# Hybrid attention layer on one core: the last query chunk's projection tiles move from the four-buffer PSUM pool "S" to the two-buffer pool "O"

## The chip, the core and the metric

The kernel runs on one core of a Trainium2 chip. The metric is the time of one execution on the device in microseconds (us). One profiled execution of the kernel before is read in detail; the rows below are from it.

## The reference, cut to what matters

One decoder layer on 512 tokens of width 1024. A normalised and modulated input `h` is projected by `w_in` into the operands of two attention groups of eight heads: NSA (query `q_n`; compressed, selected and windowed keys and values) and DSA (query `q_d`; one key and value head, and an index branch that picks 128 keys per query). Their outputs go through `w_out`, and a squared-ReLU MLP follows.

```python
h = rms_norm(x, g_pre_mix) * (1 + sc1) + sh1
proj = h @ w_in
q_n, kc, vc, ksl, vsl, kw, vw, gl, q_d, k_d, v_d, qi, ki, wi = split(proj)
k_cmp = gelu(blocks(rope(kc)) @ w1k) @ w2k          # and v_cmp from vc
o_nsa = g0 * attn(q_n, k_cmp, v_cmp) + g1 * attn_selected(q_n, ksl, vsl) + g2 * attn_window(q_n, kw, vw)
o_dsa = attn_on_topk(q_d, k_d, v_d, index(qi, ki, wi))
x = x + gt1 * rms_norm(concat(o_nsa, o_dsa) @ w_out)
x = x + gt2 * rms_norm(square(relu(h2 @ w_up)) @ w_down)
```

## The kernel before, in words

The 512 tokens are four tiles of 128 (index `t` or `j`). The columns of `w_in` are cut into chunks: A and B are projected first, together with the modulation vectors; then D, C (the NSA queries) and E (the DSA queries, "the last query chunk"). Each fp32 operand is split into a high and a low part, so a projection of one tile is 8 x 3 = 24 matmuls of 128x512 into one PSUM bank.

PSUM has eight banks, given out by `bank(tag, name)` (L112) from three pools: "S" has four buffers, "T" and "O" two each. A tile from a pool waits until the last reader of the tile that held the buffer is done. Pool "S" holds the projection tiles of D, C and E (`pj_D`, `pj_C`, `pj_E`), the index products (`ix`), the score tiles (`s_s`, `s_w`, `s_d`, and `sc` of the compressed branch), the sums `vs_g`, `gv_g`, and `cv_a`. Pool "T" holds the transposes (`skp_C`, `skp_E`, `tp_...`). Pool "O" holds, before the attention, the transposed compression inputs (`kcT`, `vcT`) and the hidden layer of the compression (`hid_k`, `hid_v`, L649), and in the attention the output accumulators `O0_j` and `O1_j` (L1124).

A tile of chunk C or E goes through four steps: `Q0` (the 24 matmuls; for E `Q0_steps`, four parts), `Q1` (ScalarE copies the bank to SBUF as `pjC` or `pjE`, L555; VectorE and GpSimd rotate one half each, L428 to L433, with the scratch `ra_C`), `Q2` (split into stacked high and low parts `sk_C`: a ScalarE cast, L437, and a GpSimd subtract, L438), `Q3` (eight transposes `skp_C` and two ScalarE copies to `qC`, L569).

The compression of the values: `kcp_v` (L643, VectorE) feeds 16 matmuls `hid_v` (L653), VectorE copies the bank out (`hx`, L660), a short chain on VectorE and ScalarE makes the GELU `hu` (L661 to L666), and `cout_v` (L674) follows. The same for the keys ends in `kcx` (L681 to L684), which `sc` (L961) reads.

The attention is a list of units (kind s, w or d; tile j). For each head a unit makes a score tile in "S" by two matmuls (L912, L913) which VectorE reads with the mask (L915, result `P_s` and the maxima `mx`), then ScalarE exponentiates (L916). Meanwhile VectorE runs the rounds of the top-k on `wk` (`MAX8` L594, `MATCH_REPLACE8` L597, 16 rounds for each of three tiles).

Where pieces of work lie in the program is set by the table `PLAN` (L41) through `place` and `slot`: chunk E at `E=(19, 2.5)` falls into the first three attention units (s of tile 0, w of tile 0, s of tile 1). The framework's scheduler then fixes the order of the instructions on each engine; each engine runs its own queue strictly in that order.

Of the kernel before, what the change touches and what calls it, by code (L numbers as in the profile page):

```python
# [69 lines left out]
def layer_kernel(  # L70
# [41 lines left out]
    def bank(tag, name, dt=F32):  # L112
        return psp.tile([P, 512], dt, tag=tag, name=name, bufs=4 if tag == "S" else 2)
# [180 lines left out]
    def mod_mm(k):  # L294
        ps, acc = macc[k]
        for v in range(2):
            mm = PE.matmul(ps[:, 256 + v:257 + v], acc[:, v, :], ones32, start=True, stop=True)
        return ps[:, 256:258], mm
# [28 lines left out]
    def proj_mm(ps, t, k, w, n):  # L327
        for i in range(3):
            proj_pass(ps, t, k, w, n, i)
# [27 lines left out]
    mp, _ = mod_mm(0)  # L357
# [105 lines left out]
    pjs, sks = {}, {}  # L463
# [81 lines left out]
    def Q0_steps(nm, t):  # L545
        def part(i):
            if i == 0:
                pjs[nm, t] = bank("S", f"pj_{nm}_{t}")
            for k in (2 * i, 2 * i + 1):
                proj_mm(pjs[nm, t], t, k, chunks[nm], 512)  # L550
        return [lambda i=i: part(i) for i in range(4)]
# [9 lines left out]
    def Q2(nm, t):  # L561
        rv = heads(pjs[nm, t], 8)
        sks[nm, t] = [stack(rv[:, g * 4:g * 4 + 4, :], 4, f"{nm}{t}{g}", G) for g in range(2)]

    def Q3(nm, t):
        q = b4(f"q{nm}_{t}", F32R).rearrange("p (h q) -> p h q", q=P)
        for g in range(2):
            ps = stack_T(sks[nm, t][g], 4, f"{nm}{t}{g}")
            A.copy(q[:, g * 4:g * 4 + 4, :], ps.rearrange("p (h q) -> p h q", q=P))  # L569
        (qn if nm == "C" else qd)[t] = q  # L570
# [224 lines left out]
    def w_in_chunk(c0, c1, nm, eng=V):  # L795
# [7 lines left out]
        def spl(i):  # L803
# [13 lines left out]
            lambda t, nm=nm: Q2(nm, t), lambda t, nm=nm: Q3(nm, t)), t) for t in range(NT) for nm in "C"]  # L817
# [53 lines left out]
    for n in range(len(tl) + 3):  # L871
# [5 lines left out]
        while mm_done < min(want, len(mm_seq)):  # L877
            f, t = tl[mm_seq[mm_done]]
# [230 lines left out]
    for n in range(16):  # L1109
# [7 lines left out]
        if prev is not None:  # L1117
            j, b = prev.j, int(prev.nm == "d")
            O = (On, Od)[b]
# [233 lines left out]
```

## Time and profile before

| quantity | value |
|---|---|
| median of 3 runs | 716.63 us (716.0 to 717.08) |
| profiled execution, its own time | 716.14 us |
| its span, first to last instruction | 714.4 us |
| outside the span | 1.7 us |
| TensorE (PE) busy / VectorE (DVE) / ScalarE (ACT) / GpSimd (POOL) | 93% / 73% / 52% / 27% of the span |
| mean granted TensorE clock | 0.977 |

PE is busy nearly all the time, but its busy time counts a matmul at half clock twice as long as one at full clock, and an idle stretch counts only where nothing runs. So the places to read are the idle stretches of PE and the stretches where the granted clock is 0.5.

### The profile page before, as it was taken

What the parts mean: (1) busy time and instruction counts of PE and PEld (TensorE: products, weight loads), DVE (VectorE), ACT (ScalarE), POOL (GpSimd) and SP (SyncE); (2) the same over time, 40 slices, a digit from 0 to 9 for tenths busy, and PEclk for the clock granted to TensorE, in tenths of its full rate; (3) what the DMA queues carried; (4) which work ended last, traced back from release to release, by engine and by line L of the source; (5) the groups of instructions that cost most, each with busy time, mean ns of one, the idle gap of its engine ahead of it and who ended that gap; (6) DMA issues with size and microseconds to landing.
All of it is one profiled execution on the core that took longest, in us unless ns stands there. A gap on an engine that the chain in (4) does not pass through costs nothing.

```text
span 714.4 us, 9896 instructions
## 1 busy us (share of the span) xinstructions
PE 662.9 (93%) x3465; PEld 519.1 (73%) x3465; DVE 522.6 (73%) x1027; ACT 371.7 (52%) x753; POOL 191.7 (27%) x228
## 2 busy tenths in 40 slices
PE   3899979989988999899978999999999999999994
PEld 2678968857665666455768878888888888888883
DVE  4557759997899999865686559657688559695535
ACT  4343784534697768644546454525545346444221
POOL 4000395624533226203010022202130022231023
PEclk9999989997999999999999999999999999999998
DMA  9998730521215421833496123361154212323103
GB/s 287 314 342 275 254 89 1 118 91 57 72 48 138 99 60 30 213 140 89 134 294 195 57 60 106 109 199 29 30 170 155 89 30 60 89 90 111 35 1 118
DMA packets 88539, 87.14 MB, mean 122 GB/s; under 512 B 3909, under 2 KB 67497, under 8 KB 88490
## 3 DMA queue, kind: packets, MB, share of 16 engines
q1 hardware_dynamic: 88098, 86.46, 40.3%
q8 instruction: 27, 0.44, 0.3%
q14 instruction: 22, 0.18, 0.1%
q10 hardware_dynamic: 392, 0.06, 0.0%
HBM read 84.40 MB, written 2.10 MB: 121 GB/s over the span
## 4 chain that ended last, share of the span: by engine, by line
PE 72%; DVE 16%; ACT 3%; DMA 3%; issue 2%; POOL 2%; DVEq 0%; POOLq 0%; ACTq 0%; SPq 0%
PE up L1154 23%; PE dn L1282 16%; PE dn L1215 5%; PE op L1045 4%; PE pA L324 3%; PE pj_E L324 3%; PE pB L324 2%; DVE wk L597 2%; PE O L944 2%; DVE m L594 2%; PE pj_D L324 1%; DMA wg_g<-in_w_ada_dram 1%; PE pj_C L324 1%; PE mp L286 1%; DVE uol_a L124 1%
## 5 line engine op out<-in xcount | busy, mean ns | idle before, releaser
L1154 PE MATMUL up<-hh,uh_U 128*128 128x512 f32 (+1 forms) x288 | 105.4, 367 | 3.2 <-ACT hh L123 2.7
L1154 PE MATMUL up<-hl,uh_U 128*128 128x512 f32 (+1 forms) x288 | 104.3, 366 | 1.5 <-DVE hl L124 1.5
L1154 PE MATMUL up<-hh,ul_U 128*128 128x512 f32 (+1 forms) x288 | 104.9, 366 | 0.0
L1244 POOL TENSOR_TENSOR r<-r,r 128x512 f32<-128x512 f32 x18 | 36.8, 2056 | 184.3 <-ACT r L1159 113.6
L123 ACT CAST th<-rd 128x1024 fp32r<-128x1024 f32 x42 | 44.2, 1053 | 75.1 <-PE dn L1282 40.7
L124 DVE TENSOR_TENSOR tl<-rd,th 128x1024 fp32r<-128x1024 f32 x42 | 54.0, 1291 | 37.8 <-ACT th L123 37.8
L124 DVE TENSOR_TENSOR ul_U<-rw_U,uh_U 128x1024 fp32r<-128x1024 f32 x32 | 43.1, 1348 | 31.2 <-ACT uh_U L123 31.1
L1154 PEld LDWEIGHTS up<-hh,uh_U 128*128 128x128 f32 x288 | 54.3, 188 | 12.7 <-ACT hh L123 3.2
L1154 PEld LDWEIGHTS up<-hl,uh_U 128*128 128x128 f32 x288 | 53.8, 189 | 10.6 <-DVE hl L124 1.7
L1154 PEld LDWEIGHTS up<-hh,ul_U 128*128 128x128 f32 x288 | 54.3, 188 | 8.7
L123 ACT CAST uh_U<-rw_U 128x1024 fp32r<-128x1024 f32 x32 | 33.6, 1049 | 49.3 <-PE up L1154 31.2
L1282 PE MATMUL dn<-th,sl 128*128 128x512 f32 x168 | 52.1, 391 | 0.3
L1282 PE MATMUL dn<-th,sh 128*128 128x512 f32 x168 | 51.9, 393 | 0.0
L1282 PE MATMUL dn<-tl,sh 128*128 128x512 f32 x168 | 51.8, 389 | 0.0
L1282 PEld LDWEIGHTS dn<-th,sh 128*128 128x128 f32 x168 | 31.5, 188 | 7.5 <-DVE usum L1269 0.6
L1282 PEld LDWEIGHTS dn<-th,sl 128*128 128x128 f32 x168 | 31.3, 188 | 7.6 <-DVE sl L124 1.2
L1282 PEld LDWEIGHTS dn<-tl,sh 128*128 128x128 f32 x168 | 31.5, 188 | 6.6
L1244 DVE TENSOR_TENSOR rd<-rd,rd 128x1024 f32<-128x1024 f32 x24 | 31.5, 1325 | 1.9 <-DMA rd<-in_w_down_dram 1.6
L123 ACT CAST sh<-r 128x512 fp32r<-128x512 f32 x42 | 25.2, 617 | 9.1 <-POOL r L1244 8.6
L124 DVE TENSOR_TENSOR sl<-r,sh 128x512 fp32r<-128x512 f32 x42 | 27.9, 713 | 0.0
L1269 DVE TENSOR_TENSOR y<-y,dn 128x512 f32<-128x512 f32 x40 | 25.5, 681 | 2.2 <-PE dn L1282 2.2
L594 DVE MAX8 m<-wk 128x8 f32<-128x256 f32 (+2 forms) x48 | 26.3, 553 | 0.8 <-POOL wk L589 0.4
(425 smaller groups left out, 1685.3 us busy)
## 6 DMA issues: line engine op xcount, KB each, us to landing
rw_U<-in_w_up_dram SPq DMA_DIRECT2D x32, 512.0 KB, 4.3
rd<-in_w_down_dram SPq DMA_DIRECT2D x24, 512.0 KB, 4.9
wm<-in_w_ada_dram SPq DMA_DIRECT2D x32, 256.0 KB, 6.1
x<-in_x_dram SPq DMA_DIRECT2D x8, 512.0 KB, 6.8
wa<-in_w_ada_dram SPq DMA_DIRECT2D x8, 512.0 KB, 7.9
wv_g<-in_w_ada_dram SPq DMA_DIRECT2D x8, 512.0 KB, 4.5
rwo_a<-in_w_out_dram SPq DMA_DIRECT2D x16, 256.0 KB, 4.3
wv_sh<-in_w_ada_dram SPq DMA_DIRECT2D x8, 512.0 KB, 3.8
```

Of the source, the lines that this page charges most:

```text
L123: A.copy(hi, src)
L124: eng.tensor_tensor(lo, src, hi.bitcast(F32), op=OP.subtract)
L324: return PE.matmul(ps[:, :n], l[:, t, k, :], r[:, k % 2, :n], start=(k == 0 and i == 0), stop=(k == KT - 1 and i == 2))
L594: mx = V.max(m8, work[t])
L597: V.match_replace(work[t], m8, work[t], MARK)
L944: mm = [PE.matmul(O[j][g * 64:(g + 1) * 64, :], vn[kb][:, self.vsl[g]:self.vsl[g] + 64], pts[kb, g][0], start=(first and kb == 0), stop=(l ...
L1045: PE.matmul(stt["ps"], l[:, kk, :], r[:, kk % 2, :], start=(kk == 0 and i == 0), stop=(kk == 7 and i == 2))
L1154: PE.matmul(pv[:, t0:t1, :], l[:, k, :], r[:, t0:t1, k, :], start=(n == 0), stop=(n == 23))
L1215: PE.matmul(ps, l[:, t * P:(t + 1) * P], r[:, f % 2, :], start=(n == 0), stop=(n == 11))
L1244: eng.tensor_tensor(dst, x, y, op=op)
L1269: V.tensor_tensor(ya, ya, ps, op=op)
L1282: PE.matmul(ps[t], l[:, f, t * P:(t + 1) * P], r[:, f, :], start=(n == 0), stop=(n == 11))
```

## The change

The bank of each `pj_E` tile is taken from pool "O" (two buffers) and no longer from pool "S" (four buffers). Nothing is computed otherwise.

```diff
     def Q0_steps(nm, t):
         def part(i):
             if i == 0:
-                pjs[nm, t] = bank("S", f"pj_{nm}_{t}")
+                pjs[nm, t] = bank("O", f"pj_{nm}_{t}")
             for k in (2 * i, 2 * i + 1):
                 proj_mm(pjs[nm, t], t, k, chunks[nm], 512)
```

The scheduler orders the instructions anew. The orders of all engines are as before up to the end of the `ix` products, and again from the second unit s of tile 0 on (apart from one or two neighbours that change places); between these PE, VectorE, ScalarE and GpSimd all run the same instructions in another order. By the waits in the built program, the first matmul of the first E tile waited before for an index bank (long free), and now waits for VectorE's copy L660 of `hid_v`, whose bank it takes; the first matmul of the second E tile waited before for a score bank, and now for the copy L660 of `hid_k`; the third takes the bank of the first, the fourth that of the second.

On PE, right after the last index products (`skp_kw_1491`), these rows stand new in front of the first E tile `pj_E_1688` (`skp_C_1534` and `skp_C_1540` are the transposes of the first C tile's halves, `s_s_0` to `s_s_3` the scores of the first four heads of the first attention unit).

```order
+L444 MATMUL skp_C_1534<-identr,sk_C_1418 128x128 x4
+L653 MATMUL hid_v<-kcp_v,w_v_905 128x62 x8
+L653 MATMUL hid_v<-kcp_v,w_v_907 128x62 x8
+L444 MATMUL skp_C_1540<-identr,sk_C_1421 128x128 x4
+L912 MATMUL s_s_0_1699<-k1s,qC_1533 128x128
+L913 MATMUL s_s_0_1699<-k2s,qC_1533 128x128
+L912 MATMUL s_s_1_1713<-k1s,qC_1533 128x128
+L913 MATMUL s_s_1_1713<-k2s,qC_1533 128x128
+L912 MATMUL s_s_2_1730<-k1s,qC_1533 128x128
+L913 MATMUL s_s_2_1730<-k2s,qC_1533 128x128
+L912 MATMUL s_s_3_1745<-k1s,qC_1533 128x128
+L913 MATMUL s_s_3_1745<-k2s,qC_1533 128x128
```

So the first E tile's 24 matmuls, which stood directly behind `skp_kw_1491` and surrounded `hid_v` and `skp_C`, now stand behind all of these.

On VectorE at the same time, right behind the rotation of the third C tile (L432 on `pjC_1473`), the copy of `hid_v` and the reads of the first scores move ahead (`wk_705` and `wk_704` are top-k work, `ra_C_1517` the rotation scratch of the fourth C tile).

```order
-L597 MATCH_REPLACE wk_705<-m_2_1672,wk_705 128x384
-L597 MATCH_REPLACE wk_704<-m_1_1675,wk_704 128x256
 L428 TENSOR_TENSOR ra_C_1517<-pjC_1515,rsin 128x4x32
 L430 TENSOR_TENSOR ra_C_1517<-pjC_1515,rsin 128x4x32
+L660 COPY hx<-hid_v 128x62
+L597 MATCH_REPLACE wk_705<-m_2_1672,wk_705 128x384
+L915 ISA P_s_1695,mx<-s_s_0_1699,mask 128x128
+L915 ISA mx 128x1
+L597 MATCH_REPLACE wk_704<-m_1_1675,wk_704 128x256
+L915 ISA P_s_1695,mx<-s_s_1_1713,mask 128x128
+L915 ISA mx 128x1
+L915 ISA P_s_1695,mx<-s_s_2_1730,mask 128x128
```

The copy of `hid_v` is now the third instruction from that point and was the eighth; the copy of `hid_k`, which the second E tile waits for, comes 25 instructions and accumulator reads behind that of `hid_v` (21 before).

On PE at the end of the third E tile (`pj_E_1814`), the sums `vs_g` close up and the two transposes of the first E tile (`skp_E_1942`, `skp_E_1948`) leave the place in front of `sc`; they come after the first two `s_w` scores now, behind `cv_a`.

```order
 L324 MATMUL pj_E_1814<-uh_E_1430,hl_173 128x512
-L749 MATMUL vs_g_1750<-wv_g_1903,c_sb 32x256
-L679 MATMUL cout_k_1626<-hu_1570,w2t_809 64x62
-L749 MATMUL vs_g_1750<-wv_g_1903,c_sb 32x256 x3
+L749 MATMUL vs_g_1750<-wv_g_1786,c_sb 32x256 x4
+L749 MATMUL vs_g_1750<-wv_g_1903,c_sb 32x256 x4
 L444 MATMUL skp_C_1654<-identr,sk_C_1582 128x128 x4
 L444 MATMUL skp_C_1660<-identr,sk_C_1585 128x128 x4
-L444 MATMUL skp_E_1942<-identr,sk_E_1808 128x128 x4
-L444 MATMUL skp_E_1948<-identr,sk_E_1811 128x128 x4
 L961 MATMUL sc_1833<-kcx,qC_1533 128x64 x8
 L827 MATMUL cv_a_1852<-ones,acc_a_187 128x1 x8
```

Between the last wide matmul of the third E tile and `cv_a` there is less narrow work than before; the fourth E tile still follows behind `cv_a`.

## Rows read from the trace of the kernel before

**Rows 1.** The page: the span, the busy time of each engine, and the shares of the chain of work that ended last.

```profile
span 714.4 us, 9896 instructions
...
PE 72%; DVE 16%; ACT 3%; DMA 3%; issue 2%; POOL 2%; DVEq 0%; POOLq 0%; ACTq 0%; SPq 0%
```

**Rows 2.** Busy time by stretch (start and end in us; length; busy us and count of PE, weight load, VectorE, ScalarE, GpSimd; granted clock; DMA share; GB/s).

```profile
150.00:160.00 10.00, 10.00 (x69) 6.60 (x68) 8.26 (x34) 3.56 (x12) 0.00 (x0) 1.00 0.43 144
160.00:170.00 10.00, 8.81 (x59) 6.65 (x57) 6.83 (x22) 4.17 (x10) 3.79 (x6) 0.98 0.38 120
170.00:180.00 10.00, 10.00 (x38) 9.09 (x39) 8.74 (x36) 3.68 (x15) 5.12 (x10) 0.51 0.00 0
180.00:190.00 10.00, 10.00 (x73) 7.64 (x75) 6.68 (x28) 5.33 (x16) 4.66 (x9) 1.00 0.01 2
```

**Rows 3.** The waits of PE over the whole span: who waited for whom, total us, times, longest us.

```profile
PE pj_E L324 <- DVE mx L915: 4.8, 1, 4.8
```

**Rows 4.** PE in order of time around the first and second E tiles (start us, us, engine, line, operation, names, shape, count, and the idle time before it with what ended it). The rows show each matmul's own time; matmuls overlap, so what one costs in a row of them is the distance from start to start.

```profile
130.41 0.28 PE L444 MATMUL skp_kw<-identr,sk_kw 128*128 128x128 f32 x2
...
133.12 1.99 PE L653 MATMUL hid_v<-kcp_v,w_v 128*128 128x62 f32 x16
134.86 0.90 PE L444 MATMUL skp_C<-identr,sk_C 128*128 128x128 f32 x8
135.59 2.05 PE L653 MATMUL hid_v<-kcp_v,w_v 128*128 128x62 f32 x16
...
139.75 0.22 PE L912 MATMUL s_s<-k1s,qC 128*128 128x128 f32 x1
...
140.14 0.45 PE L324 MATMUL pj_E<-uh_E,hh 128*128 128x512 f32 x1
...
146.00 0.80 PE L324 MATMUL pj_E<-uh_E,hh 128*128 128x512 f32 x1 [4.78 <-DVE mx L915]
146.60 0.63 PE L324 MATMUL pj_E<-ul_E,hh 128*128 128x512 f32 x1
...
148.30 0.63 PE L324 MATMUL pj_E<-uh_E,hl 128*128 128x512 f32 x1
...
149.11 0.39 PE L324 MATMUL pj_E<-ul_E,hh 128*128 128x512 f32 x1
...
151.64 0.39 PE L324 MATMUL pj_E<-uh_E,hh 128*128 128x512 f32 x1
```

**Rows 5.** VectorE in order of time, same stretch and columns.

```profile
131.79 0.68 DVE L643 TENSOR_TENSOR kcp_v<-kcp_v,peT 128x512 f32<-128x512 f32 x1
...
139.06 0.09 DVE L597 MATCH_VALUE_LOAD wk<-m,wk 128x8 f32 x1
...
139.99 0.60 DVE L428 TENSOR_TENSOR ra_C<-pjC,rsin 128x128 f32<-128x128 f32 x1
140.52 0.82 DVE L430 TENSOR_TENSOR ra_C<-pjC,rsin 128x128 f32<-128x128 f32 x1
...
142.85 0.21 DVE L660 COPY hx<-hid_v 128x62 f32<-128x62 f32 x1
...
150.06 0.21 DVE L660 COPY hx<-hid_k 128x62 f32<-128x62 f32 x1
```

**Rows 6.** ScalarE in order of time, same stretch and columns: the two halves of the first C tile, and the copy of the first E tile.

```profile
138.01 1.06 ACT L569 CAST qC<-skp_C 128x512 fp32r<-128x512 f32 x2
...
145.42 0.58 ACT L555 COPY pjE<-pj_E 128x512 f32<-128x512 f32 x1
```

**Rows 7.** The granted clock (third column from the right) in short stretches around its changes; columns as in rows 2.

```profile
146.00:149.00 3.00, 3.00 (x7) 2.43 (x8) 2.96 (x12) 1.86 (x8) 1.77 (x3) 0.50 0.00 0
164.50:169.50 5.00, 3.81 (x33) 2.60 (x32) 3.04 (x10) 2.20 (x6) 0.91 (x2) 1.00 0.32 105
169.50:179.50 10.00, 10.00 (x39) 9.16 (x39) 8.24 (x32) 4.18 (x16) 5.10 (x9) 0.50 0.00 0
179.50:180.00 0.50, 0.50 (x3) 0.43 (x2) 0.50 (x6) 0.00 (x0) 0.01 (x1) 0.74 0.00 0
```

**Rows 8.** PE in order of time at another start behind an idle stretch, in chunk C; columns as in rows 4.

```profile
103.17 0.80 PE L324 MATMUL pj_C<-uh_C,hh 128*128 128x512 f32 x1 [3.03 <-ACT rl L582]
...
107.60 0.61 PE L324 MATMUL pj_C<-ul_C,hh 128*128 128x512 f32 x1
```

**Rows 9.** PE in order of time from the last wide matmul of the third E tile to the fourth E tile; columns as in rows 4.

```profile
164.27 0.39 PE L324 MATMUL pj_E<-uh_E,hl 128*128 128x512 f32 x1
...
167.26 0.51 PE L444 MATMUL skp_C<-identr,sk_C 128*128 128x128 f32 x4 [0.77 <-ACT qC L569]
...
168.53 0.51 PE L444 MATMUL skp_E<-identr,sk_E 128*128 128x128 f32 x4 [0.42 <-ACT qC L569]
169.99 3.55 PE L827 MATMUL cv_a<-ones,acc_a 128*128 128x1 f32 x16
...
175.58 0.73 PE L324 MATMUL pj_E<-uh_E,hh 128*128 128x512 f32 x1
```

**Rows 10.** VectorE from 139 to 152 us, grouped by line and shape (count, busy us, mean ns of one, idle us before).

```profile
L597 DVE MATCH_REPLACE8 wk<-m,wk 128x384 f32<-128x384 f32 x6 | 3.3, 542 | 0.0
L594 DVE MAX8 m<-wk 128x8 f32<-128x384 f32 x5 | 2.7, 549 | 0.0
```

## The prediction

> **What bounds the kernel now.** I read the page first, for the chain that ended last: 72% of it is PE and 16% VectorE, so PE's idle and slow stretches are what can be won [rows 1]. Next the list of PE's waits: one wait of an E tile for VectorE's maxima, 4.8 us, stands in it [rows 3]. Then PE in order of time. The first E tile runs from behind `skp_kw` at 130.41 on, with `hid_v` and `skp_C` let in; its bank is read out late, because ScalarE's queue holds the copy until 145.42 [rows 4, 6]. The two scores after it sit unread in "S" while VectorE works through top-k rounds, and so the second E tile, next on PE, stands from 141.22 to 146.00 without a bank: 4.78 us [rows 4]. It then starts at half clock: steps of (148.30 - 146.60) / 4 = 0.43 us against (151.64 - 149.11) / 11 = 0.23 us, with the clock granted at 0.50 from 146 to 149 [rows 4, 7]. Last I read busy time by stretch, to see who follows: from 150 to 190 VectorE is idle for 1.74 + 3.17 + 1.26 + 3.32 = 9.5 us while PE is hardly ever idle [rows 2]. So over this region PE sets the pace, and what PE wins here VectorE can follow.
>
> **The change part by part.** No work is added or removed; the E tiles leave "S", and the scheduler reorders one region. I follow PE from the end of `skp_kw` (130.7) to where the order is as before, and count waits and half-clock time, since the work is the same.
>
> Removed: the wait of 4.78 us, and the slow start behind it. Seven matmuls at 0.43 instead of 0.23 cost 7 x 0.2 = 1.4 us [rows 4, 7]. Two small waits for ScalarE's evacuation of transposes, 0.77 and 0.42 us [rows 9], go too: `skp_C` now comes behind eight matmuls of `vs_g`, and `skp_E` behind `cv_a`. Together 7.4 us.
>
> Added, first wait: `skp_C` takes (135.59 - 134.86) / 2 = 0.37 us for four, and then `hid_v` needs `kcp_v`, which ends at 131.79 + 0.68 = 132.5 [rows 4, 5]. Before, eleven matmuls of the E tile filled this; now PE waits from 131.1 to 132.5: 1.4 us.
>
> Added, second wait: `hid_v` twice 1.74 us (134.86 - 133.12), `skp_C` 0.37 and four pairs of scores at (140.14 - 139.75) / 2 = 0.2 us each bring PE to 137.2 [rows 4]. The scores of the first four heads need only the first half of `qC`, whose copy now stands ahead of the casts on ScalarE; even at its old time, 138.01 plus half of 1.06 [rows 6], they would be done by 139.4. The first E tile then waits for the copy of `hid_v`. VectorE's queue is unchanged up to 139.06 [rows 5]; then come L428, L430 and the copy. Their old durations give 139.06 + 0.60 + 0.82 + 0.21 = 140.7; a later L428 and L430 in these rows' queue, without GpSimd on the same data, would be shorter, and at half of them the copy ends at 140.0. GpSimd does its own share of the third C tile earlier now, so I take 139.9: a wait of 2.7 us, between 2.2 and 3.5. Behind the waiting matmul on PE stand `vs_g`, the next scores and the second E tile; the top-k rounds cover VectorE meanwhile.
>
> Added, a slow start: PE has then seen 9 us of idling, transposes, 62-column and 128-column matmuls. Before, the clock fell during the 4.78 us of idling, and in another place in a stretch of narrow work that began behind the last wide matmul at 164.27 and stood at half from 169.5 [rows 7, 9]. I expect the first E tile to start at half clock. Seven slow matmuls are seen at 146.00, and eleven from 103.17 to 107.60 [rows 4, 8], so 1.4 to 2.2 us; I take nine, 1.8 us, since nothing favours either. The Trainium skill, "TensorE: Matmul & The Clock Gate", Part 1, says that the number of cold matmuls at a start varies with where in the chip's own rhythm the first one falls, and that one kernel showed 6, 11 or 14. The 7 and 11 here agree; 14 would be 2.8 us by that page, 1.0 us more than I take.
>
> The waits and slow starts so far: 1.4 + 2.7 + 1.8 - 7.4 = -1.5 us.
>
> The bank of the second E tile is freed by the copy of `hid_k`. Between the two copies stand 25 rows of VectorE's queue. Before, 21 rows took 150.06 - 142.85 = 7.2 us [rows 5]; with four more of 0.1 to 0.5 us this is 8 us, so 147.9. PE reaches that tile at 139.9 + 24 x 0.23 + 1.8 = 147.2 plus some 2.3 us of `vs_g`, three score pairs, `cout_v` and `skp_C`: 149.5. Cost nothing, with 1.6 us to spare.
>
> The second slow stretch: the clock was half from 169.5 to past 179.5, all of it with PE busy, which is half of 10.2 us, 5.1 us lost [rows 7]. It fell 5 us behind the last wide matmul (164.27 + 0.39), just as `cv_a` began, and rose some 4 us after the fourth E tile began at 175.58 [rows 9]. In the new order `skp_E` and two waits (0.73 + 0.77 + 0.42 = 1.9 us) leave the stretch between the third E tile and `cv_a`. If the clock falls as long after the last wide matmul as before, 1.9 us of the narrow work more runs at full clock and saves about half, 0.9 us; but `skp_E`, 0.73 us at full clock, moves into the slow part, while three score pairs move out behind wide matmuls. I take -0.9 us, between 0 (the clock falls that much earlier) and -1.7 (it also rises earlier, by a third of the 10.2 us).
>
> Sum: -1.5 - 0.9 = -2.4 us. From there on the order is as before, all engines have waited for PE in the region (9.5 us of slack on VectorE), and the transfers of `w_ada` and `w_out` are released by the same instructions, so the rest follows 2.4 us earlier. Against the profiled execution's own 716.14 us this is 713.7 us. That execution is 0.5 us below the median of the runs (716.63); I forecast 713.7 and leave the 0.5 us to the upper end.
>
> **The rivals.**
> *The slow stretch around `cv_a` vanishes or mostly does.* For it: PE gets there with 1.9 us less narrow work ahead of it. Against: `cv_a`, scores and `skp_E` are still some 5 us of narrow work. It would give up to 5.1 instead of 0.9: 716.14 - 1.5 - 5.1 = 709.5 us.
> *The gain is eaten.* The copy of `hid_v` comes at 140.7, the slow start takes eleven matmuls, and the second slow stretch stays as long while `skp_E` in it costs twice its 0.73 us: -1.5 + 0.8 + 0.4 + 0.7 = +0.4, thus 716.5 us, no change. The same result follows if VectorE, fully busy at 140, were the true bound of the region; its 9.5 us of idle time speak against that.
> *Slower: the second E tile waits for `hid_k`.* It depends on 25 rows of VectorE's queue, among them the GELU's tanh on ScalarE, which now stands behind four casts of C tiles that themselves wait for rotations. PE waits once that copy is later than 149.5; from 149.5 + 2.4 = 151.9 on the kernel is slower than before, by the whole delay, and beyond 153.3 by more than 0.2%. At 155 it would be 719 us. Against it: the rounds of 0.54 and 0.55 us [rows 10] ran with no idle time between them before, and 4 us of delay would need eight of them.
>
> **How the numbers follow.** Forecast (its own range 711.8 to 715.5, from the bounds of the slow start, the second wait and the second slow stretch): 0.64. Shorter slow stretch, 709.5 to 711.8: 0.10. Gain eaten, 715.5 to 717.5: 0.19. Slower: 0.07. 0.2% of 716.63 is 1.4 us, about what a measurement of this kernel can tell from no change; so faster means below 715.2 and slower above 718.1. Nearly all of the forecast and the first rival are faster: 0.72; same 0.21; slower 0.07. The range 711.0 to 716.6 leaves out the far part of the first rival and the upper ends of the others.
>
> **What the profile of the changed kernel would show.** Right: no wait of an E tile for `mx`; instead PE idle for about 1.4 us before `hid_v` and 2 to 3 us before the first `pj_E`, ended by `hx`; that tile starts near 140 with seven to eleven steps of 0.43 us; the second E tile starts near 149.5 without a wait; `cv_a` starts near 167.8 (169.99 - 1.5 - 0.73) instead of 169.99; everything behind is early by one and the same amount. Wrong: a wait of the second E tile for `hx`, a first E tile later than 141, a slow stretch behind `cv_a` longer than 10.2 us, or an early lead that is lost later.

## The result and the profile after

The changed kernel took 714.3 us (median of 20 runs), the kernel before, in the same set, 717.7 us: ratio 0.9943, 95% interval 0.9925 to 0.9962. The medians are 3.4 us apart, the ratio says about 4 us (2.7 to 5.4), where 2.4 us were forecast (713.7 against 716.14 us, a ratio of 0.9966). Two more sets of the changed kernel (below) gave 0.9952 and 0.9940. So the forecast time was 0.6 us off and its sign right, but the gain was undersized.

The execution that was profiled is the slowest of its set, 717.86 us, with a span of 716.1 us. It already reaches the last `skp_kw`, ahead of the first row that the change moves, at 133.92 us, where before it was 130.41 us [rows 4]. So I compare distances from `skp_kw`, not times from the start.

The waits of PE in the changed kernel (who waited for whom, total us, times, longest us); against [rows 3], the wait of an E tile for `mx` is gone, and two waits have come:

```profile
PE pj_E L324 <- DVE hx L660: 2.3, 1, 2.3
PE hid_v L653 <- DVE kcp_v L643: 1.5, 1, 1.5
```

PE in order of time, columns as in [rows 4]:

```profile
133.92 0.29 PE L444 MATMUL skp_kw<-identr,sk_kw 128*128 128x128 f32 x2
...
136.04 5.01 PE L653 MATMUL hid_v<-kcp_v,w_v 128*128 128x62 f32 x32 [1.50 <-DVE kcp_v L643]
140.81 0.73 PE L444 MATMUL skp_C<-identr,sk_C 128*128 128x128 f32 x4
...
145.57 0.80 PE L324 MATMUL pj_E<-uh_E,hh 128*128 128x512 f32 x1 [2.30 <-DVE hx L660]
...
148.30 0.55 PE L324 MATMUL pj_E<-uh_E,hh 128*128 128x512 f32 x1
148.69 0.39 PE L324 MATMUL pj_E<-ul_E,hh 128*128 128x512 f32 x1
...
155.20 0.47 PE L324 MATMUL pj_E<-uh_E,hh 128*128 128x512 f32 x1
...
170.64 1.93 PE L827 MATMUL cv_a<-ones,acc_a 128*128 128x1 f32 x16
...
174.25 0.76 PE L324 MATMUL pj_E<-uh_E,hh 128*128 128x512 f32 x1
```

The first E tile waits 2.30 us and takes seven slow steps (145.57 to 148.69); the second, at 155.20, waits for nothing. `cv_a` comes 36.72 us behind `skp_kw`, before it was 39.58, and its rows take 1.93 us instead of 3.55 [rows 9].

The clock in the changed kernel, by stretch (columns as in [rows 2]; a granted clock of 0.50 is the lower of its two levels, 1.2 GHz, called half clock here, and 1.00 the upper, 2.4 GHz):

```profile
138.50:148.50 10.00, 7.70 (x32) 6.93 (x32) 10.00 (x33) 3.30 (x13) 7.06 (x11) 0.50 0.35 79
148.80:172.40 23.60, 23.60 (x160) 18.77 (x158) 21.85 (x72) 8.49 (x23) 7.68 (x13) 1.00 0.32 104
172.60:179.30 6.70, 6.70 (x26) 5.83 (x27) 6.14 (x24) 3.34 (x12) 3.94 (x7) 0.50 0.06 19
```

The first slow stretch does not begin with the E tile but inside `hid_v`, and the second begins behind `cv_a`, not with it as before [rows 7].

One row then sums up the region, from `skp_kw` to the first `gv_g`; from there on the order is as before. The kernel before, then the changed kernel:

```profile
130.41:184.98 54.57, 48.60 (x277) 39.65 (x276) 45.33 (x156) 21.29 (x65) 23.45 (x35) 0.87 0.30 82
```

```profile
133.92:184.66 50.74, 46.94 (x276) 39.57 (x274) 45.53 (x156) 21.37 (x65) 23.44 (x35) 0.83 0.32 88
```

The region is 3.83 us shorter, at a lower mean clock. Behind it, from `gv_g` to the first `up` of the MLP, 172.3 us have become 173.7, at a mean clock of 0.97 against 0.99: this execution has more stretches at half clock there than the one of before, and 1.4 us are taken back. There is one profile of the kernel before, so what differs behind the region can be the luck of that one execution; the experiments come back to this.

### The profile page after: what moved, and what is told of

It is laid out like the page before. It is cut to its first block, busy times and chain, and to the rows that moved or that the text cites. A ratio compares the mean times of both kernels' runs of the same rounds, so it can differ in the third digit from the quotient of the medians.

```text
span 716.1 us, 9900 instructions
## 1 busy us (share of the span) xinstructions
PE 670.0 (94%) x3465; PEld 524.8 (73%) x3465; DVE 522.7 (73%) x1027; ACT 372.5 (52%) x753; POOL 192.2 (27%) x228
## 4 chain that ended last, share of the span: by engine, by line
PE 73%; DVE 14%; DMA 4%; issue 3%; ACT 3%; POOL 2%; SPq 0%; DVEq 0%; POOLq 0%; ACTq 0%
PE up L1154 23%; PE dn L1282 16%; PE dn L1215 5%; PE pj_E L324 4%; PE op L1045 3%; PE pA L324 3%; PE pB L324 2%; PE O L944 2%; DVE wk L597 2%; DVE m L594 2%; PE mp L286 1%; PE pj_D L324 1%; DMA rw_U<-in_w_up_dram 1%; PE tp_w L938 1%; DMA x<-in_x_dram 1%
## 5 line engine op out<-in xcount | busy, mean ns | idle before, releaser
L1244 POOL TENSOR_TENSOR r<-r,r 128x512 f32<-128x512 f32 x18 | 36.7, 2055 | 185.6 <-ACT r L1159 115.0
```

The costliest lines, as they stand in the source:

```text
L1244: eng.tensor_tensor(dst, x, y, op=op)
```

## The experiments

The theory at this point: the lead is made in the region, of three parts: fewer waits, no more split `vs_g` steps, and slow stretches that lie otherwise; what differs behind 200 us belongs to the single execution. The rivals: the waits alone; the new place of the first tile; VectorE as the true bound.

**The changed kernel again**, twice, in different sets.

> The changed kernel once more, unaltered. In its first profile the region around the E tiles gains 3.9 us (shift against the kernel before 3.5 us ahead of it, -0.4 us behind it), but slow stretches at 213 and 380 us then give back 1.3 us each. Theory: the region's gain comes again (between 3.4 and 4.4 us), and the later slow stretches belong to the one execution, so they lie elsewhere or are missing; time 0.994 of the kernel before (between 0.9925 and 0.996). Rival: the change itself brings the slow stretch at 213 us; then it stands at the same place again, and the net gain behind 230 us is at most 2.6 us.

> The changed kernel a third time, as the measure for the three others: 0.9945 of the kernel before (0.992 to 0.997). Its stretches at half clock around the E tiles are expected as before in both profiles: one that begins in hid_v, 10 us or longer, and one behind cv_a of 7 us or shorter; those behind 200 us at other places or of other lengths.

0.9952 (0.9927 to 0.9978) and 0.9940 (0.9918 to 0.9963). The region took 51.63 us in the first of these two runs and 50.78 in the second. The profile of the second repeats that of the result, the region to 0.05 us, waits and slow stretches included. In the first PE arrives ahead of ScalarE (a wait of 1.90 us for `k2w` in front of `skp_C`), the first E tile starts only 13.16 us behind `skp_kw`, and the first slow stretch is longer; its gain of 2.9 us is below the 3.4 to 4.4 expected. So the region gains 2.9 to 3.8 us each time. The slow stretch at 213 us came again in the second run at 208 us, in both cases 79.6 us behind `skp_kw`; in the first it is missing, and one stands at 230 us. So it is not luck of one execution, as the theory had it, nor is it always there. Nor is the change needed for one there, as the rival had it: the kernel with the order of before and a shorter `cv_a`, further down, has a stretch at half clock at 213.5 us, too. From `skp_kw` to the first `up` the profile of the result and these two are 2.4, 2.9 and 2.5 us shorter than that of before.

**The split steps of `vs_g`, in the order of before.**

```diff
+    for m, i in behind_vsg:
+        tc.add_manual_dep(m.ins, vsg["g1", i].ins.name,
+                          mybir.DependencyInfo(mybir.DependencyClass.NoSync, mybir.DependencyReason.DATA),
+                          reason="order")
```

`behind_vsg` holds the score of head 5, which goes behind `vs_g` step 1, and `cout_k`, which goes behind step 3. Such an order-only edge (`NoSync`) puts one instruction behind another in an engine's list and adds no wait. In this kernel lines from there on are one to three higher: L750 is L749, L913 is L912, L828 is L827.

> The kernel before (E tiles in S) with two order edges: the score of head 5 and cout_k stand behind the vs_g step that they split, everything else in the order of before. The four matmuls of a vs_g step write four groups of 32 rows; in the profile of before a step that is whole takes 0.57 us, and one that is split takes 0.55 us for each piece (two and two matmuls at 155.18 and 156.10, one and three at 164.59 and 165.40). Theory: each split costs 0.55 us, so this is 1.1 us faster than before, 0.9985, and rows show four pieces instead of six. Rival (the piece's 0.55 us is a start-up that the whole step hides elsewhere, or PE waits for something else there anyway): no change within 0.3 us; the lead seen in the changed kernel comes from waits and clock alone.

PE in order of time, before and then with the steps whole:

```profile
155.18 0.62 PE L749 MATMUL vs_g<-wv_g,c_sb 128*32 128x256 f32 x4
155.73 0.33 PE L912 MATMUL s_s<-k1s,qC 128*128 128x128 f32 x1
...
156.10 0.62 PE L749 MATMUL vs_g<-wv_g,c_sb 128*32 128x256 f32 x4
156.66 0.33 PE L912 MATMUL s_s<-k1s,qC 128*128 128x128 f32 x1
...
164.59 0.62 PE L749 MATMUL vs_g<-wv_g,c_sb 128*32 128x256 f32 x2
165.14 0.33 PE L679 MATMUL cout_k<-hu,w2t 128*64 128x62 f32 x2
165.40 0.63 PE L749 MATMUL vs_g<-wv_g,c_sb 128*32 128x256 f32 x6
165.96 0.53 PE L444 MATMUL skp_C<-identr,sk_C 128*128 128x128 f32 x4
```

```profile
157.33 0.64 PE L750 MATMUL vs_g<-wv_g,c_sb 128*32 128x256 f32 x8
157.90 0.33 PE L913 MATMUL s_s<-k1s,qC 128*128 128x128 f32 x1
...
166.06 0.64 PE L750 MATMUL vs_g<-wv_g,c_sb 128*32 128x256 f32 x8
166.63 0.33 PE L679 MATMUL cout_k<-hu,w2t 128*64 128x62 f32 x2
...
170.69 2.63 PE L828 MATMUL cv_a<-ones,acc_a 128*128 128x1 f32 x16
```

Each matmul of `vs_g` makes two rows, so x2, x4, x6 and x8 are one to four matmuls. From its start to the next row's start a piece takes 0.55 to 0.57 us whatever it holds (155.18 to 155.73, 164.59 to 165.14, 157.33 to 157.90); each split costs 0.55 us, as the theory had it. The Trainium skill, "TensorEngine Tiling (Array Packing)", Key Properties, says that independent tiles of the array work in parallel; these rows, each matmul 32 columns wide, agree. The region takes 51.68 us, 2.9 us less, of which the splits are 1.1; the rest is clock: `cv_a`, with 1.1 us less narrow work ahead of it, begins at full clock, and the mean clock of the region is 0.90 instead of 0.87. That the one follows from the other is likely, but rests on one profile. The time is 0.9979 (0.9958 to 1.0000), 1.5 us less by that ratio and near the theory's 0.9985, but with an interval that touches no change; the 1.1 us are shown by the rows, not by the time.

**Only the other three E tiles in O.**

```diff
-                pjs[nm, t] = bank("O", f"pj_{nm}_{t}")
+                pjs[nm, t] = bank("S" if t == 0 else "O", f"pj_{nm}_{t}")
```

> The first E tile stays in S, the other three take banks of O. Everything up to the second E tile runs in the order of the kernel before; hid_v's wait for kcp_v and the first tile's wait for hx do not arise. Theory (what counts is that E tiles do not wait behind unread scores; the two new waits are a pure cost of 1.5 and 2.3 us): the second E tile starts at the copy hx of hid_v, about 143.2 on the clock of the kernel before, a wait of 2 us in place of 4.78; its vs_g steps are whole in the order (none is split by a score pair), which is worth 1.3 us; with the shorter second slow stretch the gain is 4 to 6 us, 0.992 to 0.9945 of before. Rival (the gain needs the first tile moved behind the scores, since that is what empties VectorE's queue early): gain under 2 us, above 0.997.

0.9948 (0.9919 to 0.9978), just outside the 0.992 to 0.9945 of the theory and away from the rival's 0.997. The wait is 1.9 us as expected, and the region 50.9 us. Since the scheduler also reordered the stretch behind the region here, the order from the second unit s (that of tile 1) on was then held as in the changed kernel, by a chain of order-only edges on each engine; a last run moved `hx` ahead, too. (In the kernels with a held order the list stands ahead of the code, so lines are 90 higher: L750 is L660.)

> The run with the first E tile in S and the other three in O once more, but from the second attention unit s on every engine's order is held as in the changed kernel (in the first run of it the scheduler also reordered the units from 200 to 290 us and lost 2.2 us there). From the end of skp_kw to the first gv_g it took 50.9 us, the changed kernel 50.7, the kernel before 54.6. Theory (the later reordering cost those 2.2 us, and moving the first E tile is not what gains): the time is that of the changed kernel or better, 0.9915 to 0.9945 of the kernel before. Rival (the first tile's place behind the scores is needed): above 0.996.

> As the run with the order held, and the copy hx of hid_v on VectorE ahead of the rotations L428, L430, L433, the MAX8 round and L601 that stood before it (2.8 us of rows). Theory A (waits of PE add up): the second E tile's wait of 1.9 us goes to about 0.1, and the time is 1.8 us (0.0025) below the run with the order held. Theory B (the end of the region is set by the chain over the copies and rotations of C and E: skp_C waited 1.5 us there for pjE): the gain is under 0.7 us.

0.9958 (0.9934 to 0.9982) and 0.9941 (0.9910 to 0.9972): neither is told from the changed kernel's time. So the first tile's new place is not needed for the gain; without it PE runs at full clock up to `cv_a`, and the wait of 1.9 us brings no slow start, where that of 4.78 us did (the row from `skp_kw` to `cv_a` of the held run):

```profile
130.89:165.73 34.84, 30.84 (x206) 24.31 (x204) 33.93 (x113) 15.46 (x44) 17.36 (x25) 1.00 0.46 128
```

With `hx` early the 1.9 us went, but waits of `cout_v` for `hu` (1.1) and of a score for `mx` (0.7) came, and a stretch at half clock from 151.5 to 155 us; the regions are 48.85 and, held only, 48.61 us. That is the size that theory B gave, but not its mechanism: the wait of `skp_C` for `pjE`, 1.5 us in the held run, which it had as the bound, is gone as well. The medians are 1.75 us apart, as theory A had it, with intervals that overlap; so A and B are not told apart for this tile. The expected 0.9915 to 0.9945 was missed by the held run: its region was 6 us shorter than before, its time only 3 us. The 175.1 us from `gv_g` to `up`, 2.8 more than before, hold the difference.

**`hx` on ScalarE.**

```diff
-        V.tensor_copy(hx, hp[:, 0:62])
+        A.copy(hx, hp[:, 0:62])
```

> The changed kernel with the copies hx of hid_v and hid_k on ScalarE instead of VectorE. ScalarE is idle from 138.5 to 141.8 in the profile of the changed kernel, and its queue reaches the copy at 142.5; PE reaches the first E tile at 143.27. Theory (that wait of 2.3 us is on PE's path and VectorE can follow): the wait goes to under 0.5 us, and the time falls by another 1.5 to 2.3 us, to 0.991 to 0.9925 of the kernel before. Rival (VectorE, busy without a gap from 138 to 150, is the true bound of the region): the wait goes, but another takes its place and the time is that of the changed kernel, 0.994.

1.0004 (0.9983 to 1.0025): the whole gain is gone, which neither the theory nor the rival had. The wait for `hx` went; the waits of PE in the region are now

```profile
PE hid_v L653 <- DVE kcp_v L643: 1.5, 1, 1.5
PE skp_C L444 <- ACT qC L569: 0.8, 1, 0.8
PE sc L961 <- DVE kcx L684: 0.4, 1, 0.4
```

and `cv_a` stands 36.89 us behind `skp_kw`, no earlier than in the changed kernel, and begins at half clock, as in the kernel before. But the region is still 3.1 us shorter than before (51.46 us); the rest went behind it, where the order was a different one, most of it in the MLP (308.7 us from the first to the last `up`, before 303.1), in which a slow stretch of 10 us stands from 375 us on. Whether the order or the execution brings that is open. So this run says little of the wait; the next ones hold the order.

**`hx` and `kcp_v` earlier on VectorE, all else held.** In VectorE's list:

```diff
 L433 TENSOR_TENSOR pjC<-pjC,ra_C
+L660 COPY hx<-hid_v
 L594 MAX8 x2
 L586 SCALAR_TENSOR_TENSOR wk
 L432 TENSOR_TENSOR pjC<-pjC,rcos
 L428, L430 TENSOR_TENSOR ra_C
-L660 COPY hx<-hid_v
```

> The changed kernel with its own order held by order edges on PE, VectorE, ScalarE and GpSimd (they add no wait, only a sequence), and one row moved: on VectorE the copy hx of hid_v goes ahead of the two MAX8 rounds, the index sum L586 and the rotations L432, L428, L430 that stood between the end of hid_v and it (six rows, 3.7 us in the profile of the changed kernel). So unlike with the copy on ScalarE nothing later changes its place. Theory A (PE sets the pace, its waits add up): the first E tile's wait of 2.3 us goes to under 0.3, cv_a and everything behind come 2 to 2.3 us earlier, 0.9915 of the kernel before where the changed kernel has 0.9945. Theory B (the copy on ScalarE took the wait away too and cv_a came no earlier: waits for qC and kcx took its place): the wait goes, waits of skp_C or sc or vs_g behind it appear, the lead at cv_a grows by under 0.8 us, and the time is 0.9935 to 0.995.

> As the run with hx early, and the two additions kcp_v on VectorE ahead of the two MAX8 and MATCH_REPLACE8 rounds that stood before and between them (1.9 us of rows). They then end at 133.8 on the clock of the changed kernel's profile, ahead of PE's arrival at 134.4. Theory A: hid_v's wait of 1.5 us goes as well, together 3.8 us earlier than the changed kernel, 0.989 to 0.990 of the kernel before. Theory B: both waits go, but the region's end is set by the chain over VectorE and ScalarE (rotations, casts, transposes of C), so the lead behind cv_a grows by under 1 us; 0.993 to 0.995.

> The changed kernel with hx and kcp_v early on VectorE once more, unaltered, beside the changed kernel in one set of runs. It had 0.989 of the kernel before from six undisturbed runs. If that holds: 0.987 to 0.991, and 3 to 4 us below the changed kernel; if it was luck of the clock: within 1.5 us of the changed kernel.

| kernel | of before | first E tile behind `skp_kw` | region | clock |
|---|---|---|---|---|
| changed (two profiles alike) | 0.9943, 0.9940 | 11.65 us | 50.74 us | 0.83 |
| changed, PE ahead of ScalarE | 0.9952 | 13.16 us | 51.63 us | 0.83 |
| `hx` early | 0.9927 (0.9892 to 0.9961) | 11.25 us | 48.89 us | 0.86 |
| both early | 0.9890 (0.9861 to 0.9919) | 9.92 us | 48.24 us | 0.86 |
| both early, again | 0.9906 (0.9870 to 0.9942) | 8.67 us | 46.10 us | 0.96 |

Both early is the fastest kernel here: 710.6 and 711.0 us, 3.7 and 2.1 us below the changed kernel's 714.3 and 713.1 (the latter in one set). The ratios are those of theory A; the 2.1 us fall between the 3 to 4 expected of the second run and the 1.5 that would have been luck. So it is theory A in the time, but not as it was put. In the first of the two profiles the waits for `kcp_v` and `hx` are gone, with one for `sk_C` instead:

```profile
131.95 0.51 PE L534 MATMUL skp_C<-identr,sk_C 128*128 128x128 f32 x4 [1.87 <-POOL sk_C L528]
132.30 5.40 PE L743 MATMUL hid_v<-kcp_v,w_v 128*128 128x62 f32 x32
```

In the second `hid_v` runs at full clock, PE is early, and waits longer for `hx` (2.75 us) than in the changed kernel (2.30):

```profile
134.06 3.90 PE L743 MATMUL hid_v<-kcp_v,w_v 128*128 128x62 f32 x32
...
142.16 0.55 PE L414 MATMUL pj_E<-uh_E,hh 128*128 128x512 f32 x1 [2.75 <-DVE hx L750]
```

So the sum of PE's waits is no measure of the gain: narrow work at half clock and a wait behind it stand in for each other. The start of the tile is a better one: from there to the region's end the profiles of the table take 37.4 to 39.1 us, and the last of them has no second slow stretch. `hx` early alone, at 0.9927, lies between the two theories and is not told from the changed kernel by its time. Its profile is to be read against the second row, since PE was ahead of ScalarE there, too (a wait of 1.87 us for `k2w`): the tile starts 1.9 us earlier, and the region is 2.7 us shorter.

**`cv_a` cut to one product**, in both kernels, order held. The other seven products are left out, and the one column that remains stands for all eight.

```diff
-        for k in range(KT):
+        for k in range(1):
             PE.matmul(pc[:, k:k + 1], acc_a2[:, k * P:(k + 1) * P], ones[:, 0:1], ...)
```

> The changed kernel in its own order (held by order edges), with one of the eight products of cv_a left in (seven of them, 14 of its 16 rows, are left out; the first column stands for all). At full clock, as in its first profile, the rows left out took 14 x 0.112 = 1.6 us. Theory (the clock falls after a certain stretch of narrow work, cv_a is the largest part of it): the stretch at half clock behind it is shorter than 6.8 us or gone, and the gain over the changed kernel is 1.6 to 3.3 us, 0.990 to 0.992 of the kernel before. Rival (the slow stretch comes at that place whatever cv_a does): 1.6 us, 0.992, with a slow stretch as long as before.

> The kernel before in its own order (held by order edges), with the same cut of cv_a. Its rows ran at half clock here, 14 x 0.214 = 3.0 us. Theory (the change gains 1.7 us because cv_a and its neighbours leave the slow stretch): this kernel gains 3 us or more, 0.9955 or lower, and the distance to the changed kernel with the same cut shrinks from 3.9 to about 2 us. Rival (the slow stretch just falls on the next work, so that the change's gain does not hang on cv_a): it gains 1.6 us, 0.998, and the distance stays at 3.5 to 4 us.

0.9918 (0.9893 to 0.9943) and 1.0001 (0.9975 to 1.0026). From `cv_a` to `gv_g`, changed and then before, each with the cut:

```profile
166.07:176.18 10.11, 9.67 (x62) 8.36 (x62) 9.80 (x39) 5.50 (x19) 6.20 (x11) 1.00 0.24 84
```

```profile
169.48:183.64 14.16, 13.52 (x56) 11.27 (x56) 10.11 (x44) 5.88 (x22) 6.40 (x11) 0.65 0.00 0
```

The changed kernel loses its second slow stretch with `cv_a` and gains as expected. The kernel before keeps its own whole, and the cut brings nothing, which neither theory nor rival had: the distance grows where it was to shrink or stay. Together with the run of the whole `vs_g` steps, where `cv_a` began at full clock, this points to what lies ahead of `cv_a` in the order of before, the narrow work and two waits from 164.3 us on; in the new order that is less, and leaving out most of `cv_a` was enough to be rid of the stretch. Each of these rests on one profile.

## Why the prediction was right in its sign and too small

| term | predicted | measured in the region |
|---|---|---|
| waits: 5.97 us gone, two new ones | 4.1 - 5.97 = -1.9 | 3.80 - 5.97 = -2.2 |
| time lost at half clock | 1.8 - 1.4 - 0.9 = -0.5 | +0.7 |
| the matmuls themselves | 0 | -2.3 |
| sum | -2.4 | -3.8 |

The second and third lines are added up from PE's rows, start to start, to about 0.2 us: 41.97 us of work at full-clock length before, 39.70 after; 13.41 and 14.72 us spent at half clock, of which half is lost. So the mechanism that was forecast is there: a wait and a slow start go, two shorter waits and another slow start come. What was mis-sized is the time at half clock, put at -0.5 and measured at +0.7, and the matmuls themselves, put at nothing and measured at -2.3. That 714.3 lies so near to 713.7 us is luck besides: the gain was larger, and so was the time of the kernel before in that set.

**Waits: right, one of them by luck.** `hid_v` waited 1.50 us for `kcp_v` (1.4 said); the three waits for `mx` and `qC` are gone, and the second E tile starts without one, so the slower rival is out. The first E tile waited 2.30 us for `hx` (2.7 said, 2.2 to 3.5), but only because both ends of the wait came late: PE was there at 143.27, 9.35 us behind `skp_kw` where 6.8 was said (137.2), and `hx` was 2.2 us late.

**The start of the first E tile: wrong by 2.2 us.** It was to start 9.5 us behind `skp_kw` and started 11.65 behind; that is 142.1 on the clock of before, and later than 141 was one of my signs of being wrong. The step that failed is that VectorE's queue is unchanged up to L428. Its rows are, but they take longer. VectorE, and one row of GpSimd, in the changed kernel:

```profile
138.14 0.67 DVE L432 TENSOR_TENSOR pjC<-pjC,rcos 128x256 f32<-128x256 f32 x1
...
140.40 0.82 DVE L428 TENSOR_TENSOR ra_C<-pjC,rsin 128x128 f32<-128x128 f32 x1
141.14 0.28 DVE L430 TENSOR_TENSOR ra_C<-pjC,rsin 128x128 f32<-128x128 f32 x1
...
142.48 1.13 DVE L586 SCALAR_TENSOR_TENSOR wk<-rl,wi,wk 128x512 f32<-128x512 f32 x1
...
144.12 0.54 DVE L428 TENSOR_TENSOR ra_C<-pjC,rsin 128x128 f32<-128x128 f32 x1
144.58 0.81 DVE L430 TENSOR_TENSOR ra_C<-pjC,rsin 128x128 f32<-128x128 f32 x1
145.31 0.21 DVE L660 COPY hx<-hid_v 128x62 f32<-128x62 f32 x1
```

```profile
140.01 1.06 POOL L433 TENSOR_TENSOR pjC<-pjC,ra_C 128x256 f32<-128x256 f32 x1
```

I had seen that GpSimd does its half of the third C tile earlier, and counted that as relief behind 139; but it now rotates beside VectorE's rows ahead of that. L428 takes 0.82 us and ends at 141.22, just behind GpSimd's row (141.07); L430 behind it, beside an idle GpSimd, takes 0.28 us for the same size. The last rotation begins 10.2 us behind `skp_kw` (144.12), where I had it at 8.65 (139.06): 1.5 us of the 2.2. Most of the rest is that rotation itself: 1.19 us (144.12 to 145.31), where I had halved the 1.42 of before. The Trainium skill, "SBUF — State Buffer", Terms, has VectorE and GpSimd share a pair of ports that the loser waits for a whole instruction; these rows fit that. Which of the two loses can change: in the kernel before VectorE's L430 took 0.28 us beside GpSimd's L428, and that row of GpSimd was the long one.

```profile
136.75 0.28 DVE L430 TENSOR_TENSOR ra_C<-pjC,rsin 128x128 f32<-128x128 f32 x1
```

```profile
136.70 0.98 POOL L428 TENSOR_TENSOR ra_C<-pjC,rsin 128x128 f32<-128x128 f32 x1 [2.55 <-DVE wk L586]
```

**The slow start: right in its count, wrong in its place.** Seven slow steps (nine said) cost 1.4 us. But the clock had fallen 7 us earlier, inside `hid_v`: narrow work that I had named as a reason for a slow start, and costed only from the E tile on. `hid_v`'s end, four transposes and eight score products ran at half clock, which is why PE came 2.5 us late to the wait for `hx`. The late `hx` hid that: PE would only have waited longer, as it did in the second run with both copies early.

**The second slow stretch: right in direction.** 0.9 us was said, 0 to 1.7; the stretch from 172.6 to 179.3 instead of 169.5 to 179.5 is 1.7 us less lost, the far bound; in the profile with PE ahead of ScalarE it is 3.5 us long, beyond the bound. `cv_a` came 36.7 us behind `skp_kw` (37.4 said).

**"The work is the same": wrong, the largest miss.** I had the rows of the split `vs_g` steps in the order that I printed, as something that closes up, and gave them no price. Two splits are 1.1 us by the run in the order of before, 1.33 us of 3.36 in the region's rows together. The other 0.9 us are spread over other narrow rows that stand in other company, at full-clock length: `skp_E` 0.98 us before and 0.51 after, `s_s` 2.43 and 2.23, `skp_C` 3.05 and 2.87. No run took these alone, and why they are shorter is open.

**What follows behind the region: partly wrong.** "The rest follows by the same amount" holds for the order, not for the clock. 1.3 to 1.4 us were taken back there in two of three profiles of the changed kernel; of the kernels with a larger lead some gave back up to 3 us, another 0.3. From `skp_kw` to the end of the span the three profiles of the changed kernel take 582.2, 582.3 and 582.3 us, and that of before 584.0: only 1.7 us more. But that execution was one of the quicker ones of its kernel (716.14 us, the median came out at 717.7). The run with the order of before and the cut `cv_a` takes 585.7 us, with half-clock stretches at 213 and 380 us that the one profile of before lacks. So what seems taken back may well be the luck of that one profile, which is likely but not shown, and the ratio, from many runs, is the better measure of the change.

The bounds that the forecast names add up to 712.0 to 715.8 us, so its own range, 711.8 to 715.5, was a little off. With 714.3 us the rivals of a vanished slow stretch and of an eaten gain are out, though `hx` came even later than the eaten gain had it (140.7, and 142.0 on the clock of before).

## What to carry to other kernels

When a change makes the scheduler reorder, price the new neighbours too: a group of narrow matmuls that share the array cost its full time again here for each piece it was cut into, and that price stood in the rows of the kernel before. Follow the clock back to the narrow work ahead of a wide tile, not only to the tile's first matmuls, and count a wait and a slow stretch in front of the same instruction as one. An order-only edge that moves one row and holds all others tells more than an edit that lets the scheduler move everything.

## What was not expected of the hardware

- One 32-column matmul of `vs_g` takes 0.55 us and four together 0.57 us (start to start in the rows above).
- The same VectorE row of 128x128 takes 0.28 us or 0.54 to 0.82 us. The long ones stand beside rows of GpSimd; that these are the cause fits the rows, and no run took GpSimd's rows away.
- Single executions of one kernel differ by almost 1%: the changed kernel's 20 runs lie between 711.0 and 717.9 us, and its three profiles reach the last `skp_kw` at 128.5, 130.0 and 133.9 us, ahead of any changed row. Some of that is stretches at half clock that come in one execution and not in another; a single profile shows where time goes, not what a change of 0.5% is worth.
